# Weight splits moved from ScalarE to GpSimd's casting transfers, more folded sums of squares, and a new order, in a two-layer hybrid decoder trunk

## The chip, the cores and the metric

The kernel runs on one core of one Trainium2 chip. The metric is the device time of one execution in microseconds. The kernel before took 1334.37 us (median of 3 runs, 1334.32 to 1335.81).

The engines are named as the profile names them: PE is TensorE (matmuls; its weight loads stand apart as PEld), DVE is VectorE, ACT is ScalarE, POOL is GpSimd and SP is SyncE, which here only issues transfers. A transfer issued by SP and one issued by POOL stand on two different queues. Each engine works through its own instructions strictly in the order in which the program lists them.

## The reference

Two layers of the same form, all in float32, on 512 tokens of 1024 channels. Each layer normalises its input, multiplies it with one wide matrix, runs two branches (a differential attention with 8 heads, and a matrix memory, "mLSTM", with 8 heads), gates and projects both, and adds the result to its input:

```python
def hybrid_layer(x, ...):
    h = rmsnorm(x, norm_g)
    proj = h @ w_in                       # 1024 -> 10256
    aq, ak, av, az, bqk, bv, bi, bf, bo, bz, ga, gb = jnp.split(proj, idx, axis=-1)
    q = rope(rmsnorm(two_map_heads(aq), q_norm_g), cos, sin)
    k = rope(rmsnorm(two_map_heads(ak), k_norm_g), cos, sin)
    ...
    oa = diff_attention(q, k, v, lam)     # softmax(q0 k0) - lam * softmax(q1 k1), times v
    oa = rmsnorm(oa, attn_norm_g) * (1.0 - lam_init)
    ya = (oa * jax.nn.silu(az)) @ w_out_a
    qk = jax.nn.silu(causal_conv(bqk, conv_w, conv_b))
    ...
    hb = rmsnorm(mlstm_chunkwise(mq, mk, mv, i_pre, f_pre), mlstm_norm_g)
    yb = (jax.nn.sigmoid(bo) * hb * jax.nn.silu(bz)) @ w_out_b
    u = jax.nn.sigmoid(ga) * ya + jax.nn.sigmoid(gb) * yb
    return x + u @ w_o
```

## The kernel before

**Split products.** TensorE multiplies operands of a shortened format here (fp32r). To keep float32 accuracy every operand is held as two fp32r parts: `hi`, the value cast to fp32r, and `lo`, the rest (value minus hi). Each product is then three matmuls (`mm3`): hi times hi, hi times lo, lo times hi. The helper `split(hi, lo, src)` makes the parts: a cast on ACT, then a subtraction on DVE.

**Pieces of weights.** The weights are cut into pieces of 128 x 1024 floats (512 KB), 111 a layer, 222 in all (one of each layer, `gate`, is 128 x 512). A piece is `qk0` to `qk3` (four pieces each), `av`, `bv` (eight pieces each), or one of `az`, `bqk`, `bo`, `bz`, `ga`, `gb`, `woa`, `wob` (eight each); the output projection `wo` is done in 14 pieces by seven products of sums of quarters (`seven`), some of whose weights are added up by accumulating transfers of GpSimd. For a piece `load` issues a transfer on SP into a raw tile `wr` (two buffers), `prep` splits it into `wh` and `wl` (three buffers each), and the piece's function runs 24 matmuls of 512 columns with them. A buffer of `wh` is free when the last matmul that reads it is done.

**What lies between.** The heads' own work (scores, softmax, transposes, value products, decay matrices, norms) is laid between the matmuls of the pieces as events with due times. Two sums need a matmul with a matrix of ones: the norms' sums of squares (`msp_a`, `msp_b`) and the memory's denominator (`den`). Either the 128 x 512 operand is split into hi and lo and two matmuls add them up (`hi_lo`), or it is folded first (`fold`): the upper 64 partitions are added to the lower 64 on DVE, the hi and lo of the 64 rows are put one under the other in one tile, and one matmul is enough. The tables `foldA`, `foldM` and `foldD` list the heads that fold. In `qk_done` the table `qsq` lists the token tiles whose squares are summed by ACT itself, in 8 small instructions with accumulators; for the others ACT squares the tile at once and DVE reduces it. The rotation of the queries and keys (`rope`) is one multiplication with the cosines and two half-width ones with the sines.

**What sets the order.** Nothing is issued while the program is written: a `Recorder` notes every operation, and `schedule` then places them by a model of durations, due times and buffers, one list for each engine. The numbers in `TUNE` (the order of the pieces, offsets, margins, a bias for each kind of tile) steer it. All instructions are issued by one line (441 before, 445 after), so the profile is read by tile names: `wr`, `wh`, `wl` of the weights, `hh` and `hl` of the normalised input, `ws_wo` and `wt_wo` of the summed weights of the output projection, `kl` and `mql` of key and query parts that GpSimd zeroes.

Of the kernel before, what the change touches and what calls it, by code (L numbers as in the profile page):

```python
# [18 lines left out]
P = 128  # L19
# [23 lines left out]
    ),  # L43
    "qkt": 5,
    "gct": 15,
    "gls": 6,
    "glf": 5,
    "attn": (1, 5, 5, 8, 9, 13, 15, 16, 19, 24),
# [3 lines left out]
    "ml": (1, 9, 11, 12, 13, 28),  # L52
    "ahead": 3,
    "lc": 7,
    "slack": 4956.0,
    "margin": 72.0,
    "pemargin": 171.8,
    "wait": 333.1,
    "swpen": 701284048.1,
    "smargin": 51.6,  # L60
    "pwait": 0.8,
# [10 lines left out]
    "acl": 12,  # L72
    "gateA": 9,
    "gateM": 0,
    "actp": (0, 2, 3),
    "m0": 218,
    "mp": 15,
    "m4": 11,
    "slots": 20,
    "bias": {'av': 27450.0, 'msp_a': -4350.0, 'wl': 2400.0, 'wo': -3700.0, 'woh': -4650.0, 'ht': 29150.0, 'taz': -4050.0, 'ga': 16050.0, 'gt': -8800.0, 'p': -300.0, 'wo1_P': 23900.0, 'out_0_dram': -5900.0, 'p5_wo': -4950.0, 'rot': 12650.0, 'dq': -4400.0, 'oa': 450.0, 'dd': 30900.0, 'num': 20100.0, 'ld': -4700.0, 'ws1_wo': -1200.0, 'gw': -1100.0, 'hl': -350.0, 'sc': -1400.0, 'uz': -3750.0, 'mk': 7250.0, 'sbz': 550.0, 'az': 10300.0, 'posi': -650.0, 'msl_d': 1650.0, 's1_wo': 1700.0, 'wob': 50.0, 'msh_d': 6450.0, 'sq': -1600.0, 'warm': 3150.0, 'bo': -400.0, 'sdl': 200.0, 'ml': 15800.0, 'fo_b': 11200.0, 'ws0_wo': -900.0, 'wt1_wo': 1300.0, 'pb': 2000.0, 'sbo': 5350.0, 'qkt': 2000.0, 'junk': 6150.0, 'ulZ': 7650.0, 'bv': 650.0, 'bqk': -1750.0, 'uh': -3950.0, 'ms_b': -1550.0, 'gi': 1000.0, 'ob': 250.0, 'uy': 1750.0, 'gcol': -750.0, 'ms': 11250.0, 'cosv': -4100.0, 'ms_a': 1450.0, 'ones': 2450.0, 'msh_b': 6650.0, 'x1d': -1650.0, 'qt': 1100.0, 'qk0_2x': -6300.0, 'fb_a': 4650.0, 'saz': 900.0, 'xr': -2300.0, 'fb_b': 900.0, 'wo0_P': 450.0, 'qk1_0x': 1950.0, 'fb_d': -5800.0, 'msh_a': 2700.0, 'ulA': -150.0, 'ang': 150.0, 'rnh': 1400.0, 'gft': 6600.0, 'gct': 200.0, 'gc': -300.0, 'mql': -1200.0, 'rows': 150.0, 'kl': -700.0, 'posf': -150.0, 'zw': 2400.0, 'qk1_2x': -3000.0, 'gf': 450.0, 'qk0_0x': -50.0, 'uhY': 7150.0, 'qs': 3050.0, 'qy': 250.0, 'ul': -500.0, 'msl_a': 2800.0, 'uhZ': 7800.0, 'lneps': -950.0, 'gm': -4350.0, 'lq': 450.0, 'x': -3700.0, 'eps': -700.0, 'sgb': 150.0, 'wr': -400.0, 'wt0_wo': -300.0, 'stab': 8000.0, 'xn': 1200.0, 'qss': 150.0, 'den': 2000.0, 'msl_b': 950.0, 'rn': -150.0, 'glf': 900.0, 'ss': 4250.0, 'bz': -100.0, 'sdh': -200.0, 'em': -250.0, 'uhB': 850.0, 'rq': 250.0, 'sinv': -1650.0},  # L80
    "drain": 251.9,
    "risk": 295.5,
    "late": 912.7,
}


def piece_keys():
# [357 lines left out]
def kernel(ctx, tc, x, pos, wp, wg, cst, par, pb, ngb, out):  # L445
# [1034 lines left out]
    def load(i):  # L1480
# [160 lines left out]
```

## Time and profile before

| | |
|---|---|
| runs, median | 1334.37 us |
| profiled execution | 1334.56 us |
| its span, first to last instruction | 1332.5 us |
| PE busy | 1325.0 us, 99% of the span, 6200 matmuls |
| DVE busy | 1018.0 us, 76% |
| ACT busy | 907.8 us, 68% |
| POOL busy | 36.9 us, 3%, 44 instructions |
| TensorE clock granted | 1.0 |
| bytes moved | 148.14 MB, mean 111 GB/s |

How to read it: a matmul's time in the profile is longer than its distance to the next, since they overlap. The distance is what counts, and a row of many matmuls in one piece of time gives it. A row of the groups (`wh<-wr`) names the tile written, the tiles read, the count, the busy time and the mean of one; the last column is time in which the engine stood idle before them, and whom it waited for.

### The profile page before, as it was taken

What the parts mean: (1) busy time and instruction counts of PE and PEld (TensorE: products, weight loads), DVE (VectorE), ACT (ScalarE), POOL (GpSimd) and SP (SyncE); (2) the same over time, 40 slices, a digit from 0 to 9 for tenths busy, and PEclk for the clock granted to TensorE, in tenths of its full rate; (3) what the DMA queues carried; (4) which work ended last, traced back from release to release, by engine and by line L of the source; (5) the groups of instructions that cost most, each with busy time, mean ns of one, the idle gap of its engine ahead of it and who ended that gap; (6) DMA issues with size and microseconds to landing.
All of it is one profiled execution on the core that took longest, in us unless ns stands there. A gap on an engine that the chain in (4) does not pass through costs nothing.

```text
span 1332.5 us, 17532 instructions
## 1 busy us (share of the span) xinstructions
PE 1325.0 (99%) x6200; PEld 1095.0 (82%) x6200; DVE 1018.0 (76%) x1846; ACT 907.8 (68%) x1836; POOL 36.9 (3%) x44
## 2 busy tenths in 40 slices
PE   9999999999999999999999999999999999999998
PEld 7888888888888888888788888888888888888886
DVE  7898899786259968755888988997852699687566
ACT  6878798877247858743667787889762489687343
POOL 1000000000000000000200000000000000000000
PEclk9999999999999999999999999999999999999999
DMA  5222222223333443554833122222332344354646
GB/s 188 87 67 78 80 83 64 91 79 99 95 103 112 149 123 113 146 155 128 248 112 95 49 95 64 79 76 83 82 112 79 128 119 141 99 135 135 170 122 182
DMA packets 51272, 148.14 MB, mean 111 GB/s; under 512 B 6096, under 2 KB 12880, under 8 KB 51184
## 3 DMA queue, kind: packets, MB, share of 16 engines
q1 hardware_dynamic: 48880, 138.63, 32.9%
q0 software_dynamic: 2304, 8.39, 3.6%
q8 instruction: 49, 0.80, 0.2%
q14 instruction: 39, 0.32, 0.1%
HBM read 142.74 MB, written 4.26 MB: 110 GB/s over the span
## 4 chain that ended last, share of the span: by engine, by line
PE 98%; ACT 1%; DMA 0%; SPq 0%; DVE 0%; issue 0%; DVEq 0%
PE qk L441 13%; PE av L441 9%; PE az L441 7%; PE bv L441 7%; PE bqk L441 7%; PE bz L441 7%; PE bo L441 7%; PE gb L441 7%; PE ga L441 7%; PE woa L441 7%; PE wob L441 7%; PE wo_P L441 6%; PE sc L441 3%; PE num L441 2%; PE ms L441 1%; PE ut L441 1%
## 5 line engine op out<-in xcount | busy, mean ns | idle before, releaser
L441 ACT CAST wh<-wr 128x1024 fp32r<-128x1024 f32 (+1 forms) x206 | 214.8, 1045 | 190.0 <-PE ga L441 36.3
L441 DVE TENSOR_TENSOR wl<-wr,wh 128x1024 fp32r<-128x1024 f32 (+1 forms) x208 | 248.9, 1200 | 99.7 <-ACT wh L441 98.9
L441 PE MATMUL qk<-wh,hh 128*128 128x512 f32 x256 | 96.1, 401 | 0.5 <-ACT hh L441 0.5
L441 PE MATMUL qk<-wh,hl 128*128 128x512 f32 x256 | 95.3, 400 | 0.1
L441 PE MATMUL qk<-wl,hh 128*128 128x512 f32 x256 | 94.8, 396 | 0.5 <-DVE wl L441 0.5
L441 ACT ACTIVATE p<-sc,mx,rq 128x128 f32<-128x128 f32 (+3 forms) x128 | 78.8, 618 | 16.2 <-DVE mx L441 15.6
L441 PE MATMUL woa<-oa,wh 128*128 128x512 f32 x256 | 87.8, 390 | 0.0
L440 ACT ACT_TABLE_LOAD x65 | 83.4, 1283 | 1.1
L441 PE MATMUL wob<-ob,wh 128*128 128x512 f32 x256 | 83.4, 389 | 0.0
L441 PEld LDWEIGHTS qk<-wl,hh 128*128 128x128 f32 x256 | 48.0, 188 | 10.2 <-DVE wl L441 0.9
L441 PEld LDWEIGHTS wob<-ob,wh 128*128 128x128 f32 x256 | 48.1, 188 | 10.1
L441 PEld LDWEIGHTS qk<-wh,hl 128*128 128x128 f32 x256 | 48.0, 188 | 10.0 <-DVE hl L441 0.4
L441 PEld LDWEIGHTS qk<-wh,hh 128*128 128x128 f32 x256 | 47.7, 188 | 10.0 <-ACT hh L441 0.9
L441 PEld LDWEIGHTS woa<-oa,wh 128*128 128x128 f32 x256 | 47.8, 188 | 9.7
L441 DVE TENSOR_REDUCE mx<-sc 128x2 f32<-128x256 f32 (+1 forms) x64 | 52.5, 821 | 1.1
L441 PE MATMUL bqk<-hh,wl 128*128 128x512 f32 x128 | 50.3, 393 | 0.0
L441 PE MATMUL bo<-hh,wl 128*128 128x512 f32 x128 | 50.2, 392 | 0.0
L441 PE MATMUL bo<-hl,wh 128*128 128x512 f32 x128 | 50.1, 391 | 0.0
L441 PE MATMUL bo<-hh,wh 128*128 128x512 f32 x128 | 50.0, 391 | 0.0
L441 PE MATMUL bqk<-hl,wh 128*128 128x512 f32 x128 | 50.0, 393 | 0.0
L441 PE MATMUL az<-hh,wh 128*128 128x512 f32 x128 | 49.8, 397 | 0.0
L441 PE MATMUL gb<-hl,wh 128*128 128x512 f32 x128 | 49.8, 392 | 0.0
(309 smaller groups left out, 3695.9 us busy)
## 6 DMA issues: line engine op xcount, KB each, us to landing
wr<-in_wp_dram SPq DMA_DIRECT2D x204, 512.0 KB, 3.5
ws_wo<-in_wp_dram POOLq DMA_DIRECT2D x12, 512.0 KB, 6.8
dd<-rows SPq DMA_DIRECT2D x16, 256.0 KB, 4.3
em<-rows SPq DMA_DIRECT2D x16, 256.0 KB, 4.0
dd<-rows SPq DMA_DIRECT2D x16, 192.0 KB, 4.8
x<-in_x_dram SPq DMA_DIRECT2D x4, 512.0 KB, 7.4
dd<-rows SPq DMA_DIRECT2D x16, 128.0 KB, 6.0
ws_wo<-in_wp_dram SPq DMA_DIRECT2D x4, 512.0 KB, 5.2
```

Of the source, the lines that this page charges most:

```text
L440: self.tc.keep_in_program_order(self.nc.scalar.preload_act_table_set(self.SET_NAME[o["load"]]))
L441: self.tc.keep_in_program_order(getattr(o["e"], o["fn"])(*o["a"], **o["k"]))
```

## The change

It has five parts.

1. **Hi parts by GpSimd's transfers.** The pieces with places 2 to 63 of each layer, but for `gate` (61 a layer, 122 of the 222), get their `wh` by a second transfer of the same 512 KB from memory, issued by GpSimd, whose target is an fp32r tile, so that the cast is made on the way. SP's transfer into `wr` stays, and DVE's subtraction stays. ACT's cast of those pieces goes. A second way in the code (`"a"`, with an accumulating transfer for `wl`) is switched off by its table (`wa`). The buffers are as before: two `wr`, three `wh`, three `wl`.
2. **Folds.** All 8 heads of the attention fold the sum of squares (3 before), 7 of 8 of the memory (6 before) and 7 of 8 denominators (8 before). Over both layers that is 16, 14 and 14 folded sums where 6, 12 and 16 were.
3. **Squares of queries and keys.** `qsq` has one token tile instead of two: 64 small squares with accumulators on ACT become 8 wide ones, and DVE makes 8 more reductions.
4. **One-step rotation.** The two half-width multiplications with the sines become one of full width that reads the halves in reversed order: 32 instructions of 128 x 512 where 64 of 128 x 256 were.
5. **Order.** New numbers in `TUNE`, and the planner's allowance for a transfer's landing goes from 2000 to 2500 ns (4000 for reads of `rows`).

All other instructions are the same in number and kind: 6190 matmuls where there were 6200, the same 343 rows on SP, 65 table loads on ACT.

The order of the instructions shows it at three places. First GpSimd, from its first instruction of the kernel's own line on (`kl` are tiles that it zeroes, `wh2` is the hi part of piece 2, `in_wp_dram` the weights in memory). Before:

```order
L441 MEMSET kl00_0_159 64x1024
L441 MEMSET kl10_0_160 64x1024
L441 MEMSET kl00_1_279 64x1024
L441 MEMSET kl10_1_280 64x1024
L441 MEMSET kl00_2_411 64x1024
```

and after:

```order
L445 MEMSET kl00_0_159 64x1024
L445 MEMSET kl10_0_160 64x1024
L445 DMA wh2_132<-in_wp_dram 128x1024
L445 DMA wh3_139<-in_wp_dram 128x1024
L445 DMA wh4_153<-in_wp_dram 128x1024
L445 DMA wh5_156<-in_wp_dram 128x1024
```

The first weight transfer of GpSimd now stands behind two zeroings and waits for nothing else; the next wait for a free `wh` buffer.

Second PE, where the buffer of piece 0's hi part (`wh0`) is read for the last time and then taken by piece 3 (`wh3`). `qk0_0_0` to `qk0_0_3` are the results for the four token tiles; all rows are single matmuls of 512 columns. Before, from the last row that reads `wh0` to the first rows that read `wh3`:

```order
L441 MATMUL qk0_0_3_137<-wh0_112,hl0_115 128x512
L441 MATMUL qk0_0_0_134<-wh2_132,hl0_115 128x512
L441 MATMUL qk0_0_1_135<-wl2_133,hh0_114 128x512
L441 MATMUL qk0_0_1_135<-wh2_132,hl0_115 128x512
L441 MATMUL qk0_0_1_135<-wh2_132,hh0_114 128x512
L441 MATMUL qk0_0_1_135<-wl2_133,hh0_114 128x512
L441 MATMUL qk0_0_2_136<-wh1_130,hh0_114 128x512
L441 MATMUL qk0_0_1_135<-wh2_132,hl0_115 128x512
L441 MATMUL qk0_0_0_134<-wh3_139,hh0_114 128x512
L441 MATMUL qk0_0_2_136<-wl1_131,hh0_114 128x512
L441 MATMUL qk0_0_1_135<-wh3_139,hh0_114 128x512
```

and after, the last rows ahead of `wh3` and its first:

```order
L445 MATMUL qk0_0_3_137<-wl2_133,hh0_114 128x512
L445 MATMUL qk0_0_2_136<-wh2_132,hl0_115 128x512
L445 MATMUL qk0_0_3_137<-wh2_132,hl0_115 128x512
L445 MATMUL qk0_0_3_137<-wh2_132,hh0_114 128x512
L445 MATMUL qk0_0_3_137<-wl2_133,hh0_114 128x512
L445 MATMUL qk0_0_0_134<-wh3_139,hh0_114 128x512
L445 MATMUL qk0_0_1_135<-wh3_139,hh0_114 128x512
L445 MATMUL qk0_0_2_136<-wh3_139,hh0_114 128x512
```

After the change the last row that reads `wh0` stands 27 rows ahead of the first that reads `wh3` (before: 8 rows), with 26 single 512-column matmuls between them. In that stretch the buffer is free, and now GpSimd's transfer has to be made and landed in it, where before ACT's cast had to be made.

Third PE, where the first head's sum of squares is added up (`msp_a`; `msh_a` and `msl_a` are the hi and lo parts of the unfolded operand, `fo_a` the folded one). Before:

```order
L441 MATMUL qk_1_0_236<-wh_234,hl_115 128x512
L441 MATMUL qk_1_1_237<-wl_235,hh_114 128x512
L441 MATMUL msp_a_0_263<-msh_a_0_244,ones 128x512
L441 MATMUL qk_1_0_236<-wh_251,hh_114 128x512
L441 MATMUL sc_1_3_292<-qk_0x 128x512 x2
L441 MATMUL msp_a_0_263<-msl_a_0_245,ones 128x512
```

and after:

```order
L445 MATMUL qk_1_0_238<-wl_237,hh_114 128x512
L445 MATMUL qk_1_1_239<-wh_236,hh_114 128x512
L445 MATMUL qk_1_3_241<-wh_226,hl_115 128x512
L445 MATMUL msp_a_0_263<-fo_a_0_245,ones 128x512
L445 MATMUL qk_1_0_238<-wh_236,hl_115 128x512
L445 MATMUL qk_1_3_241<-wh_226,hh_114 128x512
L445 MATMUL qk_1_1_239<-wl_237,hh_114 128x512
```

One matmul on the folded tile stands where two stood.

The diff, cut to its core:

```diff
...
     "order": (
-        "qk0 av0 gate az0 qk1 az1 az2 av1 qk2 az3 az4 qk3 az6 ga3 az5 ga5 ga4 ga2 az7 bqk7 bv0 bqk4 bqk1 "
...
+        "qk0 av0 gate az0 qk1 az1 az2 av1 qk2 az3 az4 qk3 az5 ga3 az6 az7 ga2 ga4 ga5 bqk7 bv0 bqk5 ga6 "
...
     "qkt": 5,
...
-    "attn": (1, 5, 5, 8, 9, 13, 15, 16, 19, 24),
...
+    "attn": (1, 5, 5, 8, 9, 12, 15, 16, 19, 24),
...
     "ahead": 3,
...
+    "wa": (0, 0, 1, 0),
+    "wb": (2, 64, 1, 0),
+    "wahead": 5,
...
-    "qsq": (1, 3),
-    "foldA": (2, 3, 5),
-    "foldM": (0, 1, 2, 3, 4, 7),
-    "foldD": (0, 1, 2, 3, 4, 5, 6, 7),
+    "qsq": (3,),
+    "foldA": (0, 1, 2, 3, 4, 5, 6, 7),
+    "foldM": (0, 2, 3, 4, 5, 6, 7),
+    "foldD": (0, 1, 3, 4, 5, 6, 7),
...
                     size *= x
                 go = s + c if e == "POOL" else s
                 dma = max(dma, go) + size / self.rate(o)
-                end[i] = max(dma, go) + 2000.0
+                end[i] = max(dma, go) + (4000.0 if o["a"][1].tensor.name.startswith("rows") else 2500.0)
             for t in o["tiles"]:
                 r = rings[t["ring"]]
                 if not t["live"]:
...
             s4 = r2.rearrange("p (i g d) -> p i g d", i=2, g=4)
             ctab, stab = st["ctab"], st["stab"]
             V.tensor_tensor(q4, a4, ctab[:, tt].unsqueeze(2).to_broadcast([P, 2, 4, 64]), ALU.mult)
-            for hf in range(2):
-                o = 32 * hf
-                V.tensor_tensor(
-                    s4[:, :, :, o : o + 32],
-                    a4[:, :, :, 32 - o : 64 - o],
-                    stab[:, tt, :, o : o + 32].unsqueeze(2).to_broadcast([P, 2, 4, 32]),
-                    ALU.mult,
-                )
+            a5, s5_ = (x.rearrange("p (i g h d) -> p i g h d", i=2, g=4, h=2) for x in (acc, r2))
+            stb = stab[:, tt].rearrange("p i (h d) -> p i h d", h=2).unsqueeze(2).to_broadcast([P, 2, 4, 2, 32])
+            V.tensor_tensor(s5_, a5[:, :, :, ::-1, :], stb, ALU.mult)
             V.tensor_tensor(rq, rq, r2, ALU.add)
             st[("rot", tt % 2)] = rq
             if tt % 2 == 0:
...
         else:
             G.dma_start(chains[n, a], source(l, n, 1, 1 if t == "T2" else 0, a), accum_op=ALU.add)
 
+    per = len(layers[0][0])
+    def way(i):
+        key = pieces[i][1]
+        if key == "gate" or key[0] == "seven" and key[2] not in ("P1", "P2", "P3"):
+            return "s"
+        for w in "ab":
+            lo, hi, step, ph = TUNE["w" + w]
+            if lo <= i % per < hi and i % step in ((ph,) if isinstance(ph, int) else ph):
+                return w
+        return "s"
+
+    def wtile(name, dt):
+        tag = name.rstrip("0123456789")
+        return wpool.tile([P, 1024], dt, tag=tag, bufs=2 if tag == "wr" else 3, name=name)
+
+    def src_of(i):
+        l, key = pieces[i]
+        if key == "gate":
+            return wg[l]
+        if key[0] == "seven":
+            _, n, prod, a = key
+            return source(l, n, *{"P1": (0, 0), "P2": (1, 0), "P3": (1, 1)}[prod], a)
+        return wp[l, KIDX[key]]
+
     def load(i):
         if i >= len(pieces) or i in loaded:
             return
         l, key = pieces[i]
-        if key[0] == "seven":
-            _, n, prod, a = key
-            if prod in ("P1", "P2", "P3"):
-                w = wpool.tile([P, 1024], F32, tag="raw", bufs=2, name=f"wr{i}")
-                SY.dma_start(w, source(l, n, *{"P1": (0, 0), "P2": (1, 0), "P3": (1, 1)}[prod], a))
-                loaded[i] = w
+        if key != "gate" and key[0] == "seven" and key[2] not in ("P1", "P2", "P3"):
             return
-        w = wpool.tile([P, 1024], F32, tag="raw", bufs=2, name=f"wr{i}")
+        src = src_of(i)
+        if way(i) == "a":
+            wh, wl = wtile(f"wh{i}", F32R), wtile(f"wl{i}", F32R)
+            G.dma_start(wh, src)
+            A.activation(wl, wh.bitcast(F32), AF.Copy, scale=-1.0)
+            G.dma_start(wl, src, accum_op=ALU.add)
+            loaded[i] = wh
+            ready[i] = (wh, wl)
+            return
+        loaded[i] = wtile(f"wr{i}", F32)
         if key == "gate":
-            SY.dma_start(w[:, :512], wg[l])
+            SY.dma_start(loaded[i][:, :512], src)
         else:
-            SY.dma_start(w, wp[l, KIDX[key]])
-        loaded[i] = w
+            SY.dma_start(loaded[i], src)
 
     def load_sums(i):
 
...
         load(i)
         l, key = pieces[i]
         if key == "gate":
-            wh = wpool.tile([P, 1024], F32R, tag="wh", name=f"wh{i}")
+            wh = wtile(f"wh{i}", F32R)
             w4 = wh.rearrange("p (k a n) -> p k a n", k=KT, a=2)
             split(w4[:, :, 0, :], w4[:, :, 1, :], loaded[i][:, :512].rearrange("p (k n) -> p k n", k=KT))
             ready[i] = (wh, None)
             return
-        wh = wpool.tile([P, 1024], F32R, tag="wh", name=f"wh{i}")
-        wl = wpool.tile([P, 1024], F32R, tag="wl", name=f"wl{i}")
+        wh = wtile(f"wh{i}", F32R)
+        if way(i) == "b":
+            wl = wtile(f"wl{i}", F32R)
+            G.dma_start(wh, src_of(i))
+            V.tensor_tensor(wl, loaded[i], wh.bitcast(F32), ALU.subtract)
+            ready[i] = (wh, wl)
+            return
+        wl = wtile(f"wl{i}", F32R)
         if key[0] == "seven" and key[2] in ("P5", "P6", "P7", "P4"):
             _, n, prod, a = key
             load_sums(i)
...
     for i, run in enumerate(runs):
         if i in starts:
             starts[i](state["t"])
-        for a in range(3):
-            load(i + a)
+        for a in range(max(3, TUNE["wahead"])):
+            if a < 3 or i + a < len(pieces) and way(i + a) == "a":
+                load(i + a)
         for a in range(TUNE["acl"] + 1):
             load_sums(i + a)
         for a in range(TUNE["ahead"]):
...
```

More of the change, by code (lines that the diff above doesn't have):

```diff
@@ L38 @@
     "order": (
[4 rows of a table removed]
[4 rows of a table added]
     ),
     "qkt": 5,
-    "gct": 15,
-    "gls": 6,
-    "glf": 5,
-    "attn": (1, 5, 5, 8, 9, 13, 15, 16, 19, 24),
+    "gct": 10,
+    "gls": 3,
+    "glf": 7,
+    "attn": (1, 5, 5, 8, 9, 12, 15, 16, 19, 24),
     "a0": 23,
@@ L51 @@
     "a4": 7,
[L52 removed]
+    "ml": (2, 9, 12, 12, 13, 28),
     "ahead": 3,
[L54 removed]
+    "lc": 4,
     "slack": 4956.0,
     "margin": 72.0,
[L57 removed]
+    "pemargin": 225.2,
     "wait": 333.1,
[L59 to L61 removed]
+    "swpen": 5895200610.9,
+    "smargin": 0.7,
+    "pwait": 0.4,
     "wdiff": 3673.3,
     "wsp": 4,
+    "wa": (0, 0, 1, 0),
+    "wb": (2, 64, 1, 0),
+    "wahead": 5,
     "kact": (0, 2),
[L65 to L68 removed]
+    "qsq": (3,),
+    "foldA": (0, 1, 2, 3, 4, 5, 6, 7),
+    "foldM": (0, 2, 3, 4, 5, 6, 7),
+    "foldD": (0, 1, 3, 4, 5, 6, 7),
     "warm": 18,
@@ L71 @@
     "prods": 'P1 P5 P3 P6 P2 P7 P4',
[L72 removed]
+    "acl": 18,
     "gateA": 9,
[L74 removed]
+    "gateM": 4,
     "actp": (0, 2, 3),
[L76 removed]
+    "m0": 224,
     "mp": 15,
[L78 removed]
+    "m4": 23,
     "slots": 20,
[L80 removed]
@@ L84 @@
+    "drain": 447.4,
+    "risk": 247.0,
+    "late": 751.9,
 }
```

4 lines of the change are left out of this document (1 added, 3 removed), and 6 rows, old and new, of the table TUNE.

## The prediction

> **What bounds the kernel now.** I read the page first, its totals, queues and chain:
>
> ```profile
> span 1332.5 us, 17532 instructions
> PE 1325.0 (99%) x6200; PEld 1095.0 (82%) x6200; DVE 1018.0 (76%) x1846; ACT 907.8 (68%) x1836; POOL 36.9 (3%) x44
> q1 hardware_dynamic: 48880, 138.63, 32.9%
> q0 software_dynamic: 2304, 8.39, 3.6%
> PE 98%; ACT 1%; DMA 0%; SPq 0%; DVE 0%; issue 0%; DVEq 0%
> ```
>
> PE is busy 1325.0 of 1332.5 us and holds 98% of the chain that ends last. So only two things shorten the kernel: fewer matmuls, or less of the 7.5 us in which PE stands. The busy time in six stretches (start, rest of the loading phase, layer 1, the change of layers, layer 2, end) says where those are:
>
> ```profile
> core 0: us, PE busy (x) PEld busy (x) DVE busy (x) ACT busy (x) POOL busy (x), PEclk, DMA share, GB/s
> 0.00:14.00 14.00, 10.78 (x42) 7.54 (x43) 7.00 (x18) 8.90 (x17) 3.99 (x8) 1.00 0.86 302
> 14.00:36.00 22.00, 22.00 (x107) 18.18 (x106) 20.78 (x58) 13.39 (x39) 0.95 (x1) 1.00 0.32 96
> 36.00:630.00 594.00, 594.00 (x2793) 492.55 (x2792) 452.82 (x825) 415.38 (x845) 10.24 (x11) 1.00 0.33 103
> 630.00:675.00 45.00, 44.66 (x203) 35.88 (x202) 38.89 (x54) 28.78 (x43) 7.25 (x8) 1.00 0.76 227
> 675.00:1285.00 610.00, 610.00 (x2873) 505.81 (x2872) 464.95 (x849) 422.81 (x873) 11.05 (x12) 1.00 0.35 103
> 1285.00:1332.50 47.50, 43.61 (x190) 35.05 (x189) 33.55 (x46) 18.55 (x23) 3.45 (x4) 1.00 0.60 168
> ```
>
> PE stands 3.22 us in the first 14, 0.34 at the change of layers and 3.89 in the end; in the 594 and 610 us of the layers it never stands, at a granted clock of 1.00. The table of PE's waits agrees, and the chain gives the price of a matmul:
>
> ```profile
> PE warm L441 <- DVE ml L441: 1.6, 1, 1.6
> PE qk L441 <- ACT hh L441: 0.5, 1, 0.5
> PE ht L441 <- DVE junk L441: 0.5, 2, 0.3
> PE qk L441 <- DVE wl L441: 0.5, 1, 0.5
> PE wo_P L441 <- ACT wh L441: 0.3, 1, 0.3
> 468.08 14.74 PE bv L441 x65
> ```
>
> 65 matmuls in 14.74 us are 227 ns each. No wait of PE on a weight stands in the steady part; the single `wl` wait is in the start.
>
> **The change, part by part.** *Folds.* The norms and denominators took 26 + 20 + 16 matmuls and take 16 + 18 + 18 by the tables: over both layers 16, 14 and 14 of 16 sums are folded (one matmul each) where 6, 12 and 16 were, so 10 + 2 matmuls go and 2 come, 10 fewer, which is what the order has (6200 to 6190). All are of 512 columns: 10 x 0.227 = **-2.27 us**, and it counts in full since PE never stands there. A fold costs DVE more; DVE is busy 452.82 of 594 us, and these sums have slack of their own, so I take nothing (with that cover gone, a late sum delays a head's gate, not PE).
>
> *ACT's casts, squares, rotation.*
>
> ```profile
> L441 ACT CAST wh<-wr 128x1024 fp32r<-128x1024 f32 x204 | 213.6, 1049 | 189.7 <-PE ga L441 36.3 <-PE wob L441 31.6 <-PE woa L441 18.6
> L441 DVE TENSOR_TENSOR wl<-wr,wh 128x1024 fp32r<-128x1024 f32 x200 | 243.7, 1221 | 98.5 <-ACT wh L441 97.7
> L441 ACT ACTIVATE sq<-qk 128x64 f32<-128x64 f32 x128 | 27.0, 225 | 1.9 <-PE qk L441 1.3
> L441 ACT ACTIVATION_READ_ACCUMULATOR sq<-qk 128x1 f32 x128 | 25.6, 208 | 0.0
> L441 DVE TENSOR_TENSOR sq<-qk,stab 128x256 f32<-128x256 f32 x64 | 25.5, 416 | 0.3
> L441 DVE TENSOR_TENSOR rot<-qk,ctab 128x512 f32<-128x512 f32 x32 | 21.9, 684 | 0.2
> ```
>
> ACT loses 122 casts of 1.049 (128 us) and 64 small squares with their accumulators, 64 x 0.433 = 28 us, less 8 wide ones. DVE's sines go from 64 x 0.416 to 32 x about 0.684 (the cosine row of the same size): 26.6 to 21.9, 5 us less; its 8 new reductions eat most of that. All of this lies beside PE, which waits for ACT and DVE in the layers for 0.00 us. So the 156 us are worth **0**. The bound from below is the little that the casts cost where PE waited for one, 0.3 us for `wo_P<-ACT wh`, and that piece (place above 63) keeps its cast.
>
> *The transfers.* What replaces a 1.05 us cast is a transfer, and a transfer is later. The hi part can only be fetched when the buffer of the piece three places earlier is free. Before, from there to the first use a cast had to fit; now an instruction of GpSimd plus a landing. The nearest rows:
>
> ```profile
> wr<-in_wp_dram SPq DMA_DIRECT2D x204, 512.0 KB, 3.5
> ws_wo<-in_wp_dram POOLq DMA_DIRECT2D x12, 512.0 KB, 6.8
> L441 POOL DMA_DIRECT2D ws_wo<-in_wp_dram x12: 862/862/1005, 560.6 to 1307.2; - x12
> DMA to landing us min/median/max: 3.4/3.5/9.1
> DMA to landing us min/median/max: 4.4/6.1/8.4
> ```
>
> The last two are the landings of `wr` (SP) and `ws_wo` (most by GpSimd). Lower bound of the path from the issue: 3.5 for the same 512 KB, plus 0.86 of GpSimd's instruction, 4.4, which is also the shortest of the `ws_wo` row. Upper bound: the accumulating transfers' 6.1 to 6.8. They read their target as well, and stand where the DMA engines are at a share of 0.76; a cast neither adds nor stands there. I take 4.6, close to the low end.
>
> Against that stands the room that the order leaves. I counted, for each of the 122 pieces, PE's matmuls between the last use of the freed buffer and the first use of the new hi part (26 for piece 3, shown above: 26 x 0.227 = 5.9 us), less 0.2 us for the semaphores. The tightest three are 4.3 to 4.6 us, then come sixteen between 5.6 and 6.1, and the rest lie above. The lateness summed over all pieces, the lo part (1.22 us of DVE behind the landing) included, is then a function of the landing: 0.2 us at 4.4, 0.5 at 4.6, 3.8 at 5.5, 12.5 at 6.1 and 29 at 6.8. At 4.6: **+0.5 us**. So the room is just enough by plain transfers, and not by accumulating ones.
>
> DVE's subtractions wait for the landing too; what stands behind them in DVE's queue slips by as much, and PE sees that only once DVE has no slack (20.78 of 22 us busy from 14 to 36, the one stretch where it is nearly full). The raw buffer `wr` is released about 3.5 us later than with a cast; the next `wr` takes 3.5 us to land and has a whole piece's time, 24 x 0.227 = 5.4 us, so nothing.
>
> The DMA engines carry about 61 x 0.524 = 32 MB more in the first 62 pieces of a layer (roughly 340 us): 94 GB/s on top of 103. At the SP queue's price (32.9% for 138.63 MB) the share rises from 0.33 to about 0.63, at the accumulating one's (3.6% for 8.39 MB, 1.8 times dearer) to 0.87. Not full on the mean: nothing taken, part of the range.
>
> *The start.* Here is the one place where memory limits:
>
> ```profile
> 3.00:12.00 9.00, 7.62 (x30) 5.08 (x28) 4.28 (x7) 5.62 (x12) 1.64 (x2) 1.00 1.01 399
> 0.75 3.94 POOL L441 MEMSET kl<- 64x1024 f32 x4 [0.29 <-POOLq L1630]
> 2.14 5.81 DMA wr<-in_wp_dram
> 6.63 1.42 DVE L441 SCALAR_TENSOR_TENSOR junk<-x,ss,ng 128x512 f32<-128x512 f32 x2 [5.01 <-DMA ng<-in_ngb_dram]
> 7.97 1.05 ACT L441 CAST wh<-wr 128x1024 fp32r<-128x1024 f32 x1 [1.92 <-DMA wr<-in_wp_dram]
> 9.55 0.50 PE L441 MATMUL qk<-wh,hh 128*128 128x512 f32 x1 [0.55 <-ACT hh L441]
> ```
>
> From 3 to 12 us all DMA engines are busy (share 1.01, 399 GB/s). DVE waits 5.01 us for the norm's weights, ACT 1.92 for the first piece. GpSimd's first transfer, `wh2`, now stands behind two zeroings of about 1 us each and waits for nothing: it starts near 2.7 us and pours 524 KB into the full stretch, ahead of `ng` and `wr`. At 399 GB/s that is 524/399 = **+1.3 us** on what the first real matmul waits for. Bounds: 0, if these bytes stand only in for bytes that nobody waits for yet; 2.4 (1.8 times 1.3) at the accumulating price.
>
> [...]
>
> *Sum* on the profiled execution (1334.56, of which the span is 1332.5): 1334.56 - 2.27 + 0.5 + 1.3 = 1334.1; the runs' median is 0.2 below the profiled time, so **1333.9 us**, against 1334.37.
>
> **Rivals.** What a measurement tells from no change here is about 0.2%, 2.7 us: faster is below 1331.7, slower above 1337.0.
>
> *A, the forecast*: folds pay, the start takes half of it back. Its own range goes from 1332.3 (1334.56 - 2.27 - 0.2 = 1332.1, a start at 0, landings at 4.4) to 1336.5 (a start at 2.4 and 2 us of lateness, a landing near 5.1).
>
> *B, faster*: the start pays nothing, and some of the 3.22 + 3.89 us of standing at the ends goes with the new order: 1332.1, and with 1 us of the 7.1 gone 1331.1. For it: ACT, with 8.90 of 14 us busy in the start, sheds a cast there. Against: PE's waits in the start are for `ml`, `hh` and `junk`, none for that cast.
>
> *C, slower*: the casting transfers land like the accumulating ones. From a landing of 5.5 us on it decides: 1332.1 + 1.3 + 3.8 = 1337.2 there, and 1332.1 + 2.4 + 12.5 = 1347.0 at 6.1. For it: every transfer that GpSimd issued in this trace took 6.1 to 6.8 in the middle. Against: all of these accumulate.
>
> [...]
>
> [...]
>
> **How the numbers follow.** A 0.45, B 0.27, C 0.19, D 0.09. Faster 0.27 (B), the same 0.45 (A), slower 0.28 (C and D). The range goes from 1330.8 (B with 1.3 us of standing gone) to 1342.0 (half of C, all of D): it leaves out some 0.1 of C above and 0.05 of B below.
>
> **What would show it.** Folds: 6190 matmuls, and PE busy near 1322.7 plus what the start adds. ACT: `wh<-wr` x82 and some 750 us busy with the span unmoved. Landing: the row of `wh<-in_wp_dram` on GpSimd with a median near 4.6; near 6 it is C, and PE's waits then name `wh` by DMA or `wl`, above all at the pieces with the tight room. [...] Start: the first `qk` matmul at 10.9 us instead of 9.55, with `ng` landing after 6.6; at 9.55 or earlier it is B. The forecast falls if the layers' stretches show PE standing for more than 3 us, or if PE's standing in the first 15 us shrinks.

## The result

The changed kernel takes 1352.38 us (median of 4 runs, 1351.45 to 1353.85), the kernel before 1334.67 us beside it: a ratio of 1.0132 (95% interval 1.012 to 1.0145), 17.7 us slower. The forecast was 1333.9 us with a range up to 1342.0; it was wrong in kind, since "no change" was the likeliest case.

The profiled execution of the changed kernel took 1351.45 us, with a span of 1349.4 us. Its page, totals, queues and chain:

```profile
span 1349.4 us, 17531 instructions
PE 1331.8 (99%) x6190; PEld 1093.3 (81%) x6190; DVE 1028.3 (76%) x1830; ACT 793.8 (59%) x1604; POOL 101.3 (8%) x166
q0 software_dynamic: 19872, 72.36, 19.1%
PE 84%; issue 8%; DMA 4%; DVE 3%; ACT 1%; POOL 1%; SPq 0%; POOLq 0%; DVEq 0%; ACTq 0%
```

ACT is 114 us lighter, PE has its 10 matmuls fewer, and yet PE is busy 6.8 us longer and stands 17.6 us instead of 7.5. Busy time, by the same stretches (same columns as before):

```profile
0.00:14.00 14.00, 10.76 (x42) 7.76 (x42) 6.74 (x18) 8.71 (x16) 2.74 (x7) 1.00 0.89 333
36.00:630.00 594.00, 590.05 (x2758) 485.64 (x2757) 456.32 (x816) 360.86 (x747) 43.03 (x71) 1.00 0.50 152
675.00:1285.00 610.00, 604.14 (x2829) 496.54 (x2828) 466.27 (x837) 364.29 (x758) 45.17 (x75) 1.00 0.52 154
```

The start is as it was (10.76 against 10.78). In the two long stretches, where PE never stood before, it stands 3.95 and 5.86 us. What it waited for (waits of PE: waiting instruction, releaser, us in total, times, longest):

```profile
PE wob L445 <- ACT ob L445: 2.9, 2, 1.4
PE wob L445 <- DVE ob L445: 1.7, 2, 0.8
PE den L445 <- DVE fo_d L445: 1.3, 1, 1.3
PE av L445 <- ACT uh L445: 1.1, 2, 0.6
PE av L445 <- DVE wl L445: 0.9, 2, 0.6
```

None of these rows names a hi part that lands late (the `den` row has one behind it in DVE's list, as shown below). The largest is `ob`, the normalised output of the memory's last head, which `wob` multiplies: it comes late in both layers, in pieces whose casts ACT still makes. Behind that stand the clock falls (busy time of PE, granted clock, DMA share, GB/s):

```profile
574.00:576.00 2.00, 0.51 (x2) 1.00 0.53 215
576.00:580.00 4.00, 4.00 (x11) 0.57 0.72 181
```

To add it all up I took the distance from the start of each matmul to the start of the next, less the usual one of its width (227 ns for 512 columns, 174, 120 and 108 for 384, 256 and 128), from the trace's records. In us:

```
kernel                   usual  first 20 us  stands >110 ns  half clock  rest  sum
before                  1308.4          4.9             2.2         0.0  11.7  1327.2
changed                 1306.1          5.4            16.1         3.4  13.0  1344.0
difference                -2.3         +0.5           +13.9        +3.4  +1.3   +16.8
```

So the folds' 2.3 us are there; 13.9 us of new standing, at 33 places instead of 12, and 3.4 us of half clock behind the longest of them eat them. The question is what made the stands: GpSimd's transfers, one of the other parts, or the order.

### The profile page after: what moved, and what is told of

It is laid out like the page before. It is cut to its first block, busy times and chain, and to the rows that moved or that the text cites. A ratio compares the mean times of both kernels' runs of the same rounds, so it can differ in the third digit from the quotient of the medians.

```text
span 1349.4 us, 17531 instructions
## 1 busy us (share of the span) xinstructions
PE 1331.8 (99%) x6190; PEld 1093.3 (81%) x6190; DVE 1028.3 (76%) x1830; ACT 793.8 (59%) x1604; POOL 101.3 (8%) x166
## 4 chain that ended last, share of the span: by engine, by line
PE 84%; issue 8%; DMA 4%; DVE 3%; ACT 1%; POOL 1%; SPq 0%; POOLq 0%; DVEq 0%; ACTq 0%
PE qk L445 12%; PE av L445 8%; PE wob L445 7%; PE az L445 7%; PE bz L445 7%; PE gb L445 6%; PE bo L445 6%; PE wo_P L445 6%; PE bv L445 6%; PE bqk L445 4%; PE ga L445 3%; PE sc L445 3%; DMA wh<-in_wp_dram 3%; PE num L445 2%; PE woa L445 2%
## 5 line engine op out<-in xcount | busy, mean ns | idle before, releaser
L445 DVE TENSOR_TENSOR wl<-wr,wh 128x1024 fp32r<-128x1024 f32 (+1 forms) x206 | 249.1, 1210 | 96.5 <-DMA wh<-in_wp_dram 47.4
L445 ACT CAST wh<-wr 128x1024 fp32r<-128x1024 f32 (+1 forms) x84 | 87.3, 1040 | 105.0 <-PE wob L445 22.3
L445 POOL DMA_DIRECT2D wh<-in_wp_dram x122 | 64.6, 530 | 750.5 <-PE qk L445 101.3
L445 PE MATMUL woa<-oa,wh 128*128 128x512 f32 x256 | 82.3, 390 | 0.0
L445 DVE SCALAR_TENSOR_TENSOR cv<-bqk,par,cv 128x509 f32<-128x509 f32 (+2 forms) x48 | 35.8, 746 | 22.3 <-ACT cv L445 21.5
L445 ACT CAST uh<-ut 128x128 fp32r<-128x128 f32 (+2 forms) x80 | 29.6, 370 | 39.0 <-PE ut L445 32.0
L445 PE MATMUL ga<-hh,wh 128*128 128x512 f32 x128 | 50.6, 398 | 0.0
L445 PE MATMUL az<-hh,wl 128*128 128x512 f32 x128 | 50.5, 400 | 0.0
L445 PE MATMUL az<-hl,wh 128*128 128x512 f32 x128 | 50.2, 397 | 0.0
```

The lines of the kernel that those rows point to most:

```text
L445: self.tc.keep_in_program_order(getattr(o["e"], o["fn"])(*o["a"], **o["k"]))
```

## The experiments

Each run is compared with the kernel before on the same chip.

**First four: transfers or order?** `e1` holds the changed kernel's lists and gives the 122 casts back to ACT; `e2` and `e3` put the planner's allowances back; `e4` takes the transfers away and lets the planner lay the lists anew.

`e1`, in the loop that issues (the lists of PE, DVE and SP are row by row those of the changed kernel):

```diff
         for i in order:
             o = self.ops[i]
+            if o["eng"] == "POOL" and o["fn"] == "dma_start" and o["a"][0].tensor.name.startswith("wh"):
+                casts[i] = min(self.at[j] for j in users[i]) - 1300.0
+                continue
+            for j in [j for j in casts if j in o["pre"] or o["eng"] == "ACT" and self.at[i] >= casts[j]]:
+                casts.pop(j)
+                self.tc.keep_in_program_order(self.nc.scalar.copy(self.ops[j]["a"][0], self.ops[j + 1]["a"][1]))
```

`e2`; `e3` has 2000.0 for all in the same line:

```diff
-                end[i] = max(dma, go) + (4000.0 if o["a"][1].tensor.name.startswith("rows") else 2500.0)
+                end[i] = max(dma, go) + (2000.0 if o["a"][1].tensor.name.startswith("rows") else 2500.0)
```

`e4`:

```diff
-    "wb": (2, 64, 1, 0),
+    "wb": (0, 0, 1, 0),
```

> The changed kernel with its lists held: PE, DVE and SP have the same instructions in the same places, but the 122 hi parts are cast by ScalarE again (a cast is put into its list about 1.3 us ahead of the first use) and GpSimd's 122 transfers are gone. Theory 'order' (the new lists themselves make PE stand, whoever makes the hi parts): the time stays within 3 us of 1352, and the stand of PE ahead of the wob matmuls of the last head (1.4 + 0.8 us in each layer) stays. Theory 'transfers' (late landings, or DVE held up by them, cost the 17.6 us): back to 1334 to 1338.

> The changed kernel, its planner's allowance for the landing of reads of 'rows' put back from 4000 to 2000 ns, the 2500 ns for all other transfers kept. It changes only the order. Theory 'order': the stand ahead of the last head's wob matmuls goes (two times about 2.7 us of standing and about 2 us of slow clock behind it), so 9 us less, 1343. Theory 'transfers': within 2 us of 1352.

> The changed kernel with the planner's old allowance of 2000 ns for every transfer. All 122 transfers of GpSimd stay. Theory 'order': PE stands less at every place where a list was laid for a landing that comes sooner: 10 to 15 us less, 1337 to 1342. Theory 'transfers': the planner now leaves less room for each landing, so the same or slower, 1352 to 1360.

> The changed kernel without GpSimd's transfers: all hi parts by ScalarE, and the planner lays the order anew with all other new numbers. Theory 'order': about as slow as the changed kernel, 1350 to 1354. Theory 'transfers': 1334 to 1338, with 2.3 us gained by the folds perhaps 1332.

```
run                      us, median    ratio to before (95%)
e1 lists held, ACT casts   1375.42     1.0305 (1.0290 to 1.0321)
e2 rows 2000               1355.78     1.0158 (1.0143 to 1.0174)
e3 all 2000                1353.97     1.0132 (1.0111 to 1.0153)
e4 no transfers            1351.10     1.0123 (1.0108 to 1.0138)
```

`e4` speaks for the order: without any of GpSimd's transfers the kernel is only 1.3 us faster than the changed one, and 16.5 us slower than the kernel before. Its largest wait is the same, to the tenth (waits of PE):

```profile
PE wob L445 <- ACT ob L445: 2.9, 2, 1.4
PE sc L445 <- ACT p L445: 2.2, 4, 0.9
PE ga L445 <- ACT ua L445: 1.8, 2, 0.9
PE wob L445 <- DVE ob L445: 1.7, 2, 0.8
```

`e1` gives neither theory's time. The `wob` stand stayed (2.9 and 1.7 us), as 'order' had it, but lists made for an ACT without these casts get 122 casts, and PE then waits for ACT's and DVE's other work (`sc` for `p` 5.8 us, `qkt` for `kl` 4.3). So this run doesn't tell transfers and order apart. `e2` missed both numbers, and `e3` came out where 'transfers' had it (1352 to 1360). In `e2` the `wob` stand went, as expected, and others came in its place. DVE's waits for transfers in `e2` say why:

```profile
DVE wl L445 <- DMA wh<-in_wp_dram: 49.4, 23, 5.6
DVE dd L445 <- DMA dd<-rows: 9.4, 6, 2.4
```

Reads of `rows` do land late: DVE, which works through its list in order, stands 9.4 us for them (1.1 us in the changed kernel), and PE behind it at `ms` and `msp_a`. The larger allowance for `rows` is nearer to what the traces show. But the two longest stands at `den` (1.43 and 1.88 us idle) come behind hi parts that landed 7.1 and 7.5 us after their issue, and in `e3` five stands of PE, 7.7 us in all beyond the usual distances, come behind hi parts that landed 5.9 to 8.1 us after theirs. So in these two runs late transfers cost time as well.

**Next four: one part alone, and lists held.** The one-step rotation is the smallest part: it only takes work away. `e5` puts it alone into the kernel before, and the planner lays the lists anew with the old numbers. `e6` puts it into the lists of the kernel before, the first half-width multiplication dropped, the second widened in place. `e7` and `e8` are the changed kernel with the old `foldM`, `e8` also without transfers for pieces 2 to 7 of each layer.

`e5` has the rotation's lines of the change (shown with the diff) and nothing else. `e6` records the two old multiplications for the planner and issues the new one:

```diff
+            rec.merge[len(rec.ops) - 1] = (s5_, a5[:, :, :, ::-1, :], stb, ALU.mult)
...
+            if i + 1 in self.merge:
+                continue
             o = self.ops[i]
+            if i in self.merge:
+                o["a"], o["k"] = self.merge[i], {}
```

`e7` has the first pair of lines, `e8` both:

```diff
-    "foldM": (0, 2, 3, 4, 5, 6, 7),
+    "foldM": (0, 1, 2, 3, 4, 7),
...
-    "wb": (2, 64, 1, 0),
+    "wb": (8, 64, 1, 0),
```

> The kernel before with one part of the change alone, the one-step rotation: 32 instructions of DVE fewer, some 5 us of its busy time. The planner lays all lists anew, with the numbers of before. Theory 'lists' (the numbers fit one program only; whatever is changed in it, the planner lays other lists, in which PE stands): 8 to 13 us slower than before, 1343 to 1347, with PE standing at places that have nothing to do with the rotation. Theory 'parts' (each part costs or gains by what it does itself): 1333 to 1335.

> The same rotation, but the lists are those of the kernel before, instruction by instruction: the first of the two half-width multiplications is left out, the second becomes the full-width one in its place. Theory 'lists': no change, 1333.5 to 1335. Theory 'parts', if the rotation alone was slow in the run beside this one because the reversed read is slow: as slow as there.

> The changed kernel with the old list of folded memory sums (heads 0, 1, 2, 3, 4, 7 instead of 0, 2 to 7), so two heads less late in the chain of the last heads; all 122 transfers stay. If the late wob matmuls come from the longer chain of the folded heads 5 and 6, the stand there goes and with it the slow clock behind it: 8 to 10 us less, 1343. If it is the transfers that are late there: no change, 1350 to 1354.

> The same, and GpSimd's transfers only from piece 8 of each layer on (56 instead of 62 places), so that none stands in the start and in the first pieces of a layer. If the transfers cost at the start of the two layers, where the room was counted as tightest (pieces 3, 5, 6 and 113 to 118), 3 to 5 us less than the run beside it, 1339; if they cost nothing there, within 1 us of it.

```
run                         us, median    ratio to before (95%)
e5 rotation, lists anew       1347.09     1.0088 (1.0073 to 1.0103)
e6 rotation, lists held       1335.25     1.0003 (0.9994 to 1.0013)
e7 foldM as before            1348.95     1.0105 (1.0088 to 1.0122)
e8 and transfers from 8 on    1351.30     1.0121 (1.0106 to 1.0136)
```

The pair `e5` and `e6` settles what the rotation does: nothing by itself (1.0003), and 12.3 us through the order. One place shows how. In `e5` the longest wait of PE is 2.93 us in layer 1 (timeline of PE, then of DVE: start, us, instruction, and the idle time before it):

```profile
216.21 0.40 PE L441 MATMUL ga<-hl,wh 128*128 128x512 f32 x1
219.53 0.51 PE L441 MATMUL az<-hh,wl 128*128 128x512 f32 x1 [2.93 <-DVE wl L441]
```

```profile
217.09 0.67 DVE L441 TENSOR_TENSOR rot<-rot,sq 128x512 f32<-128x512 f32 x1
217.79 0.43 DVE L441 TENSOR_TENSOR qs<-qkt,qs 64x256 fp32r<-64x256 f32 x1
218.25 1.23 DVE L441 TENSOR_TENSOR wl<-wr,wh 128x1024 fp32r<-128x1024 f32 x1
```

The row is the lo part of piece 30. It is issued late, not slow. In the list of before the same row stands right behind the scaling of the second rotated tile of the head and runs at 212.00 (timeline of DVE):

```profile
211.67 0.41 DVE L441 TENSOR_TENSOR rot<-rot,rq 128x256 f32<-128x256 f32 x1
212.00 1.22 DVE L441 TENSOR_TENSOR wl<-wr,wh 128x1024 fp32r<-128x1024 f32 x1
```

In `e5` six more rows (three steps of the next tile's rotation, three small splits) stand between that scaling and the subtraction. The planner places at each moment the most urgent row that its model holds ready. That fewer instructions ahead made other rows ready at other moments is the likely reason; it was not traced in the planner. The row's hi part was there long before: ACT's cast of it ended at 212.6. DVE has no more to do there than before (8.59 of 9.5 us busy from 210 in `e5`, 8.93 of 9.5 from 206 before); what differs is what stands ahead of the row.

`e7` took the `wob` stand away, as its first theory had it, but so did `e2` with all folds in place, so the stand belongs to the lists and can't be put on the folds of heads 5 and 6. And the time fell by 3.4 us only, not 8 to 10: new stands took part of the gain (`ms` for `dd` 1.6 us, `den` for `fo_d` 1.4), and the start another 2.0 (`qk` waits 2.5 us for `hh`, 0.5 in the changed kernel). `e8` missed both its numbers: without the transfers at the start of the layers PE stood elsewhere (waits of PE):

```profile
PE den L445 <- DVE fo_d L445: 5.2, 2, 3.2
```

Both of these stands come behind a hi part that DVE waited for, landed 7.7 and 8.8 us after its issue.

**Third four: the order by itself, and fitted numbers.** `e12` is the cleanest: the kernel before with nothing but the changed allowance, not one instruction more or less. `e11` is the kernel before with the new fold lists. `e9` and `e10` are the changed kernel, without and with the transfers, the planner's biases and margins fitted anew to exactly that program by trying small changes of them against the planner's own span.

`e12`, against the kernel before:

```diff
-                end[i] = max(dma, go) + 2000.0
+                end[i] = max(dma, go) + (4000.0 if o["a"][1].tensor.name.startswith("rows") else 2500.0)
```

`e11`, against the kernel before:

```diff
-    "foldA": (2, 3, 5),
-    "foldM": (0, 1, 2, 3, 4, 7),
-    "foldD": (0, 1, 2, 3, 4, 5, 6, 7),
+    "foldA": (0, 1, 2, 3, 4, 5, 6, 7),
+    "foldM": (0, 2, 3, 4, 5, 6, 7),
+    "foldD": (0, 1, 3, 4, 5, 6, 7),
```

`e9` against the changed kernel, with `bias`, `margin`, `pemargin` and the other margins replaced by fitted numbers (`e10` likewise, with the transfers, 4000 for `rows` and for GpSimd, 2500 else):

```diff
-    "wb": (2, 64, 1, 0),
+    "wb": (0, 0, 1, 0),
...
-                end[i] = max(dma, go) + (4000.0 if o["a"][1].tensor.name.startswith("rows") else 2500.0)
+                end[i] = max(dma, go) + (2800.0 if o["a"][1].tensor.name.startswith("rows") else 2000.0)
```

> The changed kernel without GpSimd's transfers (folds, squares and rotation kept), the planner's biases and margins fitted anew to this very program, allowances 2000 ns (2800 for rows). Nothing but the order differs from the run e4_no_transfers (1351.1). Theory 'lists': the stands of PE go and the 10 matmuls saved show: 1330.5 to 1333.5. Theory 'parts' (the folds, squares or rotation themselves cost): 1345 or more.

> The changed kernel with all its parts, the 122 transfers among them, biases and margins fitted anew with an allowance of 4000 ns for GpSimd's transfers and for rows (2500 for SP's others), since single landings took 7 us. Theory 'lists': most of the 17.7 us come back, 1337 to 1342; what stays over e9_no_transfers_refit is what the transfers cost with lists made for them. If the transfers cost by themselves whatever the lists: 1350 or more.

> The kernel before with the three fold lists of the change alone (10 matmuls fewer), all other numbers as before, so the planner lays the lists anew. Theory 'lists': 1345 to 1350 in spite of 2.3 us less work for PE. Theory 'parts': 1332.

> The kernel before, with the planner's allowance for landings of the changed kernel alone (2500 ns, 4000 for rows, instead of 2000). Not one instruction differs in kind or number, only the order. Theory 'lists': 1345 to 1350. Theory 'parts': 1334 to 1336.

```
run                             us, median    ratio to before (95%)
e9 no transfers, fitted           1342.75     1.0057 (1.0045 to 1.0070)
e10 all parts, fitted             1345.94     1.0083 (1.0069 to 1.0097)
e11 folds alone                   1354.21     1.0145 (1.0131 to 1.0159)
e12 allowance alone               1349.76     1.0108 (1.0093 to 1.0124)
```

`e12` costs 15.0 us with the same instructions. Its waits of PE are of the kind seen in the changed kernel, a last head that is late at `wob`:

```profile
PE wob L441 <- ACT sgb L441: 2.8, 2, 1.4
PE wob L441 <- ACT ob L441: 1.8, 2, 0.9
PE ut L441 <- DVE p L441: 1.4, 1, 1.4
```

`e11` costs 19.4 us, more than the 10 to 15 expected, though PE has less to do. `e10` came out between its theories (1337 to 1342, or 1350 and more). `e9` gave back half of the loss and fell short of what 'lists' expected: in it DVE stood for late reads of `rows` and PE behind it, at four places (waits of DVE, then of PE):

```profile
DVE dd L440 <- DMA dd<-rows: 9.3, 6, 2.7
```

```profile
PE msp_a L440 <- DVE fo_a L440: 3.8, 2, 2.5
PE den L440 <- DVE fo_d L440: 2.9, 2, 1.4
```

So the fit had used an allowance that these reads don't keep.

**Last three: fitted with the landings that the traces show.**

`e13` (without transfers) against the changed kernel, with fitted biases and margins; `e14` likewise with 4500 and 2200; `e15` has the transfers and 5000 for `rows`, 4500 for GpSimd, 2500 else:

```diff
-    "wb": (2, 64, 1, 0),
+    "wb": (0, 0, 1, 0),
...
-                end[i] = max(dma, go) + (4000.0 if o["a"][1].tensor.name.startswith("rows") else 2500.0)
+                end[i] = max(dma, go) + (5000.0 if o["a"][1].tensor.name.startswith("rows") else 4000.0 if e == "POOL" else 2400.0)
```

> As e9_no_transfers_refit (folds, squares and rotation, no transfers of GpSimd, numbers fitted anew), but fitted with an allowance of 5000 ns for reads of 'rows' and 2400 for other transfers, since in e9_no_transfers_refit DVE stood up to 2.7 us for a read of rows and PE behind it at four places. Theory 'lists': these four stands (8 us with the slow clock) go, 1331.5 to 1334.5, no slower than the kernel before. If the folds themselves make the memory's chain too long for any list: 1340 or more, with PE standing at den and msp_a again.

> The same with 4500 and 2200 ns, another fit. Theory 'lists': 1331 to 1335; the run beside it and this one differ only in where single late reads still meet the lists. If the folds themselves cost: 1340 or more.

> All parts, the 122 transfers among them, fitted with 5000 ns for rows, 4500 for GpSimd's transfers, 2500 for the rest. If what is over in e10_all_parts_refit (1345.9) came from too early lists: 1338 to 1342. If the transfers hold DVE whatever the lists: within 2 us of 1345.9. The difference to the two runs beside it is what the transfers cost with lists made for them.

```
run                             us, median    ratio to before (95%)
e13 no transfers, rows 5000       1333.34     0.9991 (0.9982 to 1.0000)
e14 no transfers, rows 4500       1332.68     0.9985 (0.9976 to 0.9994)
e15 all parts, rows 5000          1344.08     1.0068 (1.0054 to 1.0082)
```

`e13` and `e14` have every part but the transfers, the change's order of the pieces among them, and the loss is gone, as 'lists' had it. `e14` is 2.0 us under the kernel before, clear by its interval, and about what 10 matmuls are worth (2.27); but the lists of the kernel before were not fitted anew in the same way, so that this gain is the folds' is not shown. The long stretches of `e13` are full again (594 and 610 us):

```profile
36.00:630.00 594.00, 593.85 (x2793) 492.40 (x2792) 458.34 (x818) 412.05 (x802) 10.41 (x11) 1.00 0.36 103
675.00:1285.00 610.00, 609.48 (x2869) 505.11 (x2868) 469.70 (x841) 418.63 (x815) 11.05 (x12) 1.00 0.35 102
```

`e15`, with the transfers, stays 11 us above these two, within 2 us of `e10`, as its second theory had it. The same sum of distances shows where (us):

```
kernel      usual  first 20 us  stands >110 ns  half clock  rest
e12        1308.4          4.8            14.5         2.2  12.5
e13        1306.1          5.0             4.0         0.0  11.0
e14        1306.1          5.5             2.7         0.0  12.1
e15        1306.1          7.1            10.4         0.4  13.3
```

Between `e15` and the two others, some 7 us are stands past the start and 2 us the start, which holds 3.41 us of half clock from 13.0 us on in `e15`. Only one of these stands is seen directly behind a hi part (waits of PE):

```profile
PE bqk L440 <- DMA wh<-in_wp_dram: 0.3, 1, 0.3
```

That transfer landed 10.0 us after its issue. The other stands of over 0.3 us wait for work of ACT and DVE with no transfer just ahead of it, as in `e12`. So most of the 11 us are what these lists cost, and that the transfers themselves cost them is not shown.

**What a transfer does to the lists.** In the changed kernel the landings of the hi parts (the row of the issues with its median, then the landings of the tile) are good in the middle, better than I had taken, and bad at the end:

```profile
wh<-in_wp_dram POOLq DMA_DIRECT2D x122, 512.0 KB, 4.0
```

```profile
DMA to landing us min/median/max: 3.7/4.0/7.7
```

What DVE waits for at `wl` in the kernel before, then in the changed one:

```profile
DVE wl L441 <- ACT wh L441: 104.5, 46, 8.8
```

```profile
DVE wl L445 <- ACT wh L445: 48.8, 31, 5.8
DVE wl L445 <- DMA wh<-in_wp_dram: 47.4, 24, 5.7
DVE dd L445 <- DMA dd<-rows: 1.1, 1, 1.1
```

It stands 47.4 us for transfers of hi parts, but no longer for hi parts as a whole: 96.2 us, where it stood 104.5 for ACT's casts before. What counts is what lies behind such a wait. Three landings in the layers took over 6 us (7.7, 7.7 and 6.9), each issued within 3.3 us of the last of four reads of `rows`, and behind each of them PE stands, at `msp_a`, `msp_a` and `den`: 0.4, 0.4 and 1.4 us beyond the usual distances, 2.2 of the 16.1 us of stands. One case in layer 2, picked rows from the timeline of all engines:

```profile
1058.49 2.10 SPq L445 DMA_DIRECT2D dd<-rows  x4
1063.85 0.53 POOL L445 DMA_DIRECT2D wh<-in_wp_dram x1 [5.58 <-PE woa L445]
1068.52 0.62 ACT L445 CAST fo_d<-dd 64x512 fp32r<-64x512 f32 x1 [0.75 <-DVE dd L445]
1070.79 1.23 DVE L445 TENSOR_TENSOR wl<-wr,wh 128x1024 fp32r<-128x1024 f32 x1 [2.31 <-DMA wh<-in_wp_dram]
1072.05 0.68 DVE L445 TENSOR_TENSOR fo_d<-dd,fo_d 64x512 fp32r<-64x512 f32 x1
1072.79 0.50 PE L445 MATMUL den<-fo_d,ones 128*128 128x512 f32 x1 [1.27 <-DVE fo_d L445]
```

The transfer is issued at 1063.85; by the trace's records its first packet moves 4.8 us later, and it lands after 6.9. SP's queue moves the four reads of `rows` in that time, in packets of 512 to 2048 bytes. Busy time from 1062 to 1071 (columns as in the stretches above):

```profile
1062.00:1064.00 2.00, 2.00 (x10) 1.65 (x9) 1.54 (x3) 1.27 (x1) 0.15 (x1) 1.00 1.02 298
1064.00:1067.50 3.50, 3.50 (x18) 2.88 (x17) 3.05 (x5) 0.35 (x1) 0.38 (x1) 1.00 0.26 61
1067.50:1071.00 3.50, 3.50 (x19) 3.02 (x18) 0.89 (x2) 0.89 (x2) 0.00 (x0) 1.00 0.77 296
```

While they drain, 61 GB/s move at a share of 0.26, and neither GpSimd's transfer nor, until 1067, the `wr` on SP begins. The subtraction then stands at the head of DVE's list, `fo_d` (0.68 us of work, its input ready at 1069.1) stands behind it, and PE waits 1.27 us for `den`. Why GpSimd's packets don't start earlier while the engines are three quarters idle was not settled.

## Why the prediction was wrong

**The step that failed** is one that the sum never had. The change's fifth part, the new order, was listed among the parts and not priced, and the parts beside PE were priced at 0 because PE "waits for ACT and DVE in the layers for 0.00 us". That reading was of the lists of before. It says that in those lists every row stands in time; it does not say that the engines have room for any list. DVE is busy 76% of the span, ACT 68%, and PE's rows need hundreds of theirs in time. With other lists, and with not one other instruction (`e12`), PE stands and the kernel loses 15.0 us. In the changed kernel this is +13.9 us of standing and +3.4 of half clock, and only 2.2 us of the standing come directly behind late landings. The prediction's own sign came: PE stands for more than 3 us in each of the layers' stretches (3.95 and 5.86). The order of the changed kernel could be read before the result, and I read it for the room of the hi parts only.

Step by step:

- *Folds, -2.27 us*: right. 6190 matmuls, -2.3 in the sum of distances; with fitted lists and no transfers the kernel is 1.3 (`e13`) and 2.0 us (`e14`) faster, though the fit may have a part in that. "These sums have slack of their own, so I take nothing" was right about the work and wrong about the lists that came: `e11`, the folds alone with the old numbers, costs 19.4 us, and `e14` gains with the same folds.
- *ACT's casts and squares, worth 0*: right in kind. ACT is 114 us lighter, not 156 (793.8; I had said some 750). Nearly all of that is the casts: `e4`, which keeps them, is at 906.4 against 907.8 before, so the 28 us for the squares were too much, and the folds add work on ACT that I didn't count (`e11`, the folds alone, is at 914.7).
- *Rotation, worth 0 in its own work*: right, 1.0003 with lists held (`e6`).
- *Landing, 4.6 us*: the median is 4.0, and GpSimd's instruction takes 0.53, not 0.86. PE's list of waits names no hi part. No run shows the 0.2 us for semaphores: from the end of PE's matmul to GpSimd's start it is 0.30 in the median of 75 waits, and 0.02 from a landing to DVE. Rival C falls: the accumulating price (6.1 to 6.8) does not show in the middle of the landings. *D*, a GpSimd held up in its issuing, which has 0.09 of the chances and a part in the upper end of the range, is shown by no run: of the 122 issue rows of the changed kernel the first took 0.69 us and the others 0.53 to 0.55, and their mean is 530 or 531 ns in the six other kernels with these transfers too. The +0.5 us took one landing for all; it is the three late ones that cost, 2.2 us, where DVE has other work behind the subtraction.
- *"PE sees that only once DVE has no slack"*: wrong in its condition. DVE is busy 76% of the span, and it stood for hi parts as long before (104.5 us) as now (96.2). It is single rows queued behind a late one that have no slack, at `den` and `msp_a`. With lists fitted to each, the kernel with transfers is about 11 us slower (`e15` against `e13` and `e14`). Whether that is the transfers' doing or the fit's, and whether lists exist that hide them better, is open: the fit is a search that was stopped, not exhausted.
- *Start, +1.3 us*: an estimate, 524 KB at the 399 GB/s measured there; that the first real matmul pays for all these bytes is shown by no run. In the changed kernel it pays nothing, with the first `qk` matmul at 9.52 against 9.55. In the five other kernels that issue `wh2` at the same place it comes at 10.7 to 11.1, in the eleven without it (the kernel before among them) at 9.55 to 10.25. The mean of all six is 10.7, of the eleven 9.9: a term of about 0.8, each from one profile.
- *The rivals*: none was the one that happened. The planner, which lays all lists anew from any change, was told of in the part on the kernel, and it was the mechanism to price.

That lists alone can cost this much is shown by `e12` and by `e5` against `e6`, and that folds, squares and rotation need cost nothing by `e13` and `e14`. How the 17.7 us of the changed kernel split between the new numbers and the transfers is not shown: `e4` takes 1.3 us off without transfers, but in lists laid anew, and of the numbers that set the order only the allowance was run alone.

## What to carry to other kernels

Where a static order holds a full engine together, "the engine never waits" belongs to that order, not to the kernel: a change that re-lays it must be priced by reading the new lists, asking at each place where PE needs a result what now stands ahead of it on the in-order engines. To learn what an edit itself is worth, hold the lists and change only the instruction; to learn what it can be worth, fit the planner's numbers again to the changed program, with the landings that the trace shows. A transfer in the place of a cast takes work from one engine and puts its worst landing (7.7 us here), not its median (4.0), at the head of another one's queue.

## What was not expected of the hardware

The clock fell to half behind short stands of PE. The longest ones of the changed kernel (1.59 and 1.11 us with one matmul between them) were followed by eight matmuls at 427 ns instead of 227, a granted clock of 0.57 from 576 to 580 us; this costs 1.6 us more in each layer. In `e2` a stand of 2.05 us had six such matmuls behind it. A stand of 1.44 us in the changed kernel had none, but neither had one of 2.96 us in `e3`, and in `e1` the same pair as in the changed kernel (1.59 and 1.11 us) is followed by five in layer 1 and by none in layer 2. So the length alone does not decide. (A stand's length is here the distance of two matmuls beyond the usual one.)

Eight matmuls at 427 ns make 3.4 us, 8 x 0.2 = 1.6 us more than at 227. A stand of 2.05 us was enough for six of them in `e2`. So, as an estimate from these runs, a stand of 2 us in a full engine is to be priced with up to 1.6 us on top. What decides whether the clock falls, where the same stand of `e1` has the effect in one layer and not in the other, was not shown.
